# Two encoder layers on one core: gates through a logarithm, background steps at quarter tiles, an earlier operand split, and three narrow products for one projection

## The chip, the cores and the metric

The kernel runs on one core of a Trainium2 chip. The metric is the device time of one launch in microseconds (us). The kernel before takes 2427.96 us, the median of 3 runs (2427.77 to 2428.14).

## The reference, cut to what matters

Two layers of a bidirectional hybrid encoder work on 272 rows (16 meta rows and 256 tokens), model width 2048, in float32. Each layer is

```python
proj = h @ w_in          # gla q,k,v,r | low-rank decay | na q,k,v
o    = gated linear attention of q,k,v (4 heads, both directions)
o    = o * rsqrt(mean(o*o) + eps) * norm_w * silu(r)
y_na = neighbourhood attention (16 heads, softmax over a local window and the meta rows)
h    = LN(alpha*h + concat(o, y_na) @ w_out)
h    = LN(alpha*h + square(relu(h @ w_ff1)) @ w_ff2)
```

with `silu(r) = r / (1 + exp(-r))`. The meta rows are dropped at the end, so in layer two the columns that nothing else needs (gla q, r, na q and everything from the output projection on) are computed for 256 rows, not 272.

## The kernel before, in words

**Layout and products.** Activations lie with features on the 128 partitions and the 256 or 272 rows along the free axis. Each float32 matrix product is made of rounded parts: a weight chunk is split into a high part `wh` (a ScalarE cast, L147) and a low part `wl` (a VectorE subtraction, L148), an activation into `xh` and `xl`, and the sum is wh·xh + wh·xl + wl·xh. Weights stream from HBM in tiles of 128x1024, eight chunks each, issued by SyncE (L146) and always prepared two tiles ahead.

`by_m` (L190) makes one output tile of 128 features at a time: 16 chunks of 128 input features (32 in the second feed-forward product), each through `three` (L151). For 256 columns `three` issues two matmuls per chunk: wh against xh and xl side by side, 512 columns into a whole PSUM bank (L156), then wl against xh, 256 columns added to the right half (L157). The two halves of the bank must then be summed, in `whole` (L164): a ScalarE copy of the right half (L169), then a VectorE addition of the left half (L170), through the one buffer `jn`. For 272, 274 or 258 columns `three` issues three matmuls that add up in one region (L160 to L162), and nothing has to be summed.

**Two queues of side work.** While the big products run, generators are advanced by `pump` (L104): `fg` (foreground: silu of the gates, neighbourhood attention of a head pair, layer norm) and `bg` (background: gated linear attention). Each call adds credits and takes as many steps as whole credits are there. `by_m` calls it twice per tile, after chunk 8 and after the tile is taken out of PSUM; the rates of a call are `(1, GLA_R=1.3)` while the eight gate tiles `r` are made (L266) and `(1, GLA_NA=1.1)` during the 24 tiles of neighbourhood attention (L269). Before the last group of those, what is left of `bg` is run at once (L270). A planner (the tile framework's) lays the instructions of each engine in one order at build time; each engine runs its queue strictly in that order. Every side step's VectorE instructions are placed behind the newest `wl` (L98).

**Gated linear attention** (`gla`, L479) handles 4 heads, 10 levels each. One step of a level: TensorE multiplies the level's operands (L505, L498 and L500 for level 9) into a bank; the operands of the next level are made, an `Exp` on ScalarE (L471) and a multiplication on VectorE (L476, or L473 and L474); and GpSimd makes the differences for the level after that (`gaps`, four subtractions L460, or L447 to L450 for level 9). The buffers `lev` are three deep, so GpSimd may start a level's differences only when TensorE is through with the level three earlier. After the levels `gla_out` (L529) splits the 16 meta rows `Am` into the stack `am` (a memset L533 on GpSimd, two casts L214 on ScalarE, a subtraction L215 on VectorE) and, in its next steps, multiplies for each of two halves (L542 to L544, of which L544 reads `am`). Then come the mean of squares (L776), Newton's root and the output, which needs `gate`.

**Gates** (`ev_r`, L406, and `silu`, L417): ScalarE makes exp(-r) (L411), GpSimd adds 1 (L412), ScalarE copies r (L414); then three foreground steps: nothing, VectorE's reciprocal of each half (L421), and the product `gate` (L424). The buffers `rs` and `rv` are two deep.

Of the kernel before, what the change touches and what calls it, by code (L numbers as in the profile page):

```python
# [2 lines left out]

# [28 lines left out]
EPS = 1e-5  # L32
TAU = 16.0
NEG = -1e30
GLA_R, GLA_NA, NORMS = 1.3, 1.1, (1.0, 0.6)
LEAD = 4


# [9 lines left out]
class Trunk:  # L48
# [18 lines left out]
    def consts(self):  # L67
        nc, c = self.nc, self.cp
        t = lambda n, s, d=F32: c.tile(s, d, name=n, tag=n)
        self.vec = t("vec", [P, DEPTH, 66])  # L70
        nc.sync.dma_start(self.vec, self.i["vec"].rearrange("l p v -> p l v"))
        self.ident = t("ident", [P, P])
        nc.sync.dma_start(self.ident, self.i["ident"])
        self.sel = t("sel", [LRK, 2])
        nc.sync.dma_start(self.sel, self.i["sel"])
        self.qmask = t("qmask", [NM, NK2])
        nc.sync.dma_start(self.qmask, self.i["qmask"])
        self.mask = t("mask", [P, 7, P], U8)
# [12 lines left out]
        nc.gpsimd.memset(self.eps, EPS)  # L91
        self.one = t("one", [P, 1])
        nc.gpsimd.memset(self.one, 1.0)

# [53 lines left out]
            self.wl = nc.vector.tensor_tensor(wl[:, c], raw[:, c], wh[:, c].bitcast(F32), ALU.subtract).ins  # L148
        return wh, wl

    def three(self, ps, wh, wl, c, x, n, first, last):  # L151

        mm = self.nc.tensor.matmul
        xh, xl = x
        if n == T:
            mm(ps, lhsT=wh[:, c:c + P], rhs=x.both[:, :, :T], start=first, stop=False)  # L156
            mm(ps[:, T:], lhsT=wl[:, c:c + P], rhs=xh[:, :T], start=False, stop=last)  # L157
# [32 lines left out]
    def by_m(self, acts, ns, evict, pump=(0, 0), apart=False, renew=False):  # L190

        nk = len(acts)
        for m, n in enumerate(ns):
            ps = self.pm.tile([P, 512], F32, name="mm", tag="mm")
            for k in range(nk):
                if k % 8 == 0:
                    wh, wl = self.weights()
                self.three(ps, wh, wl, (k % 8) * P, acts[k], n, k == 0, k == nk - 1)
                if k % 8 == 7 and k < nk - 1:
                    self.pump(*pump)  # L200
                if renew and m == len(ns) - 1 and k == 8:
                    self.renew(2)
            parts = [ps[:, :T], ps[:, T:]] if n == T else [ps[:, :n]]
            evict(m, parts if apart else self.whole(parts))
            self.pump(*pump)

    def split(self, src, hi, lo):
        self.nc.scalar.copy(hi, src)
# [13 lines left out]
    def layer(self, l):  # L222
        nc, tc = self.nc, self.tc
        self.l = l
        self.full = l + 1 < DEPTH
        self.n = n = L if self.full else T
        with ExitStack() as actx:
            pool = lambda name, side, ctx=actx, bufs=1: ctx.enter_context(
                tc.tile_pool(name=name, bufs=bufs, side=side, reuse_waits="tile"))
            a = pool("att", "left")  # L230
            t = lambda nm, s: a.tile(s, F32, name=nm, tag=nm)
            self.qk = [t(f"qk{h}", [P, 2, L]) for h in range(GH)]
            self.be = [t(f"be{h}", [P, 2, L + 1]) for h in range(GH)]
            self.V = [t(f"V{i}", [P, GH * GDV]) for i in range(2)]
            self.VS = a.tile([80, GH * GDV], F32R, name="VS", tag="VS")
            nc.gpsimd.memset(self.VS.bitcast(F32), 0.0)
            self.y, self.gate, self.done = [None] * DC, {}, set()
            if l:
                self.by_m(self.x, [L + 2] * 4, lambda m, ps: self.fixed(self.ev_k, m, ps), pump=(1, NORMS[0]),
                          renew=True)  # L240
                first = self.by_k(self.x, L, self.normed)
                self.drain()
                self.lctx.close()
            else:
                with ExitStack() as ectx:
                    self.xr = pool("xr", "right", ectx)
                    for m, ps in enumerate(self.by_k(self.x, L, self.load_x, fine=True)):
                        self.ev_k(m, ps)
            with ExitStack() as ectx:
                self.ep = pool("early", "right", ectx)  # L250
                self.fcredit = 0
                self.fg.append(self.gates())
                if l == 0:
                    self.by_m(self.x, [L] * 4, self.ev_v, pump=(1, 0))
                else:
                    for m, ps in enumerate(first):
                        self.ev_v(m, ps)
                self.by_m(self.x, [n] * 4, self.ev_q, pump=(1, 0))
                self.by_m(self.x, [L] * 4, lambda m, ps: self.ev_v(4 + m, ps), pump=(1, 0))
                self.drain()  # L260
            self.a2 = pool("na", "left", bufs=2)
            with ExitStack() as gctx:
                self.credit = 0
                self.g2 = pool("gla", "right", gctx, 2)
                self.bg.append(self.gla())
                for g in range(2):  # L266
                    self.by_m(self.x, [n] * 4, lambda m, ps: self.ev_r(4 * g + m, ps), pump=(1, GLA_R))
                self.na_tiles()
                for g in range(6):  # L269
# [136 lines left out]
    def ev_r(self, c, ps):  # L406

        nc, n = self.nc, self.n
        self.y[c] = self.pair(self.yp, "y", c)
        s = self.g2.tile([P, L], F32, name="rs", tag="rs")[:, :n]  # L410
        nc.scalar.activation(s, ps, AF.Exp, scale=-1.0)  # L411
        nc.gpsimd.tensor_scalar(s, s, 1.0, 1.0, ALU.mult, ALU.add)  # L412
        r = self.g2.tile([P, L], F32, name="rv", tag="rv")[:, :n]
        nc.scalar.copy(r, ps)  # L414
        self.fg.append(self.silu(c, s, r))

    def silu(self, c, s, r):  # L417
        yield
        half = self.n // 2
        for p in (slice(0, half), slice(half, self.n)):  # L420
            self.nc.vector.reciprocal(s[:, p], s[:, p])  # L421
            yield
        gate = self.g2.tile([P, L], F32, name=f"gate{c}", tag=f"gate{c}", bufs=1)[:, :self.n]
        self.nc.vector.tensor_tensor(gate, r, s, ALU.mult)  # L424
        self.gate[c] = gate

    def newton(self, y, v, eps, t):
        nc = self.nc
# [50 lines left out]
    def gla(self):  # L479
# [11 lines left out]
        for h in range(GH):  # L491
            A = g2.tile([P, 6, P], F32, name="A", tag="A")
            Am = g2.tile([NM, L], F32, name="Am", tag="Am")
            for lv in levels:
# [19 lines left out]
                if lv == 9:  # L514
                    if full:
                        nc.vector.tensor_copy(A[:, 2:6:3, :NM], ps[:, T:T + 2 * NM].rearrange("p (s c) -> p s c", s=2))
                    nc.scalar.copy(Am[:, :T], ps[:NM, :T])
                elif lv >= 7:
                    nc.scalar.copy(A[:, 0:5:4, :] if lv == 7 else A[:, 1:4:2, :], p2)
                else:  # L520
# [6 lines left out]
            yield from self.gla_out(h, A, Am)  # L527

    def gla_out(self, h, A, Am):  # L529

        nc, n, g2 = self.nc, self.n, self.g2
        am = g2.tile([80, L], F32R, name="am", tag="am")[:, :n]
        nc.gpsimd.memset(am.bitcast(F32), 0.0)  # L533
        self.stack(Am[:, :n], am, NM, (0, 64), 32)
        yield
        af = A.rearrange("p s c -> p (s c)")
        os_ = []
# [485 lines left out]
```

## Time and profile before

| what | value |
|---|---|
| median of the runs | 2427.96 us |
| the profiled execution | 2427.82 us |
| its span, first to last instruction | 2425.8 us |
| mean granted TensorE clock | 0.997 |
| gate tiles, layer one / layer two, about | 113 to 171 us / 1345 to 1403 us |
| neighbourhood attention, layer one / layer two, about | 171 to 366 us / 1403 to 1591 us |
| `wl` subtractions L148, mean of 772 | 1226 ns |
| `wh` casts L147, mean of 772 | 1044 ns |

The profile has one page per execution and a trace that answers questions: a group of instructions by line, stretches of time with the busy time of each engine, and a timeline, whose rows are a start (us from the first instruction), a duration, an engine and line, the operation, and in brackets how long the engine had been idle and what ended that. Matmuls are pipelined, so their durations overlap: what a matmul costs is the distance from its start to the next one's start. All source lines named are those of the kernel before.

### The profile page before, as it was taken

What the parts mean: (1) busy time and instruction counts of PE and PEld (TensorE: products, weight loads), DVE (VectorE), ACT (ScalarE), POOL (GpSimd) and SP (SyncE); (2) the same over time, 40 slices, a digit from 0 to 9 for tenths busy, and PEclk for the clock granted to TensorE, in tenths of its full rate; (3) what the DMA queues carried; (4) which work ended last, traced back from release to release, by engine and by line L of the source; (5) the groups of instructions that cost most, each with busy time, mean ns of one, the idle gap of its engine ahead of it and who ended that gap; (6) DMA issues with size and microseconds to landing.
All of it is one profiled execution on the core that took longest, in us unless ns stands there. A gap on an engine that the chain in (4) does not pass through costs nothing.

```text
span 2425.8 us, 43082 instructions
## 1 busy us (share of the span) xinstructions
PE 2394.4 (99%) x17276; PEld 2270.6 (94%) x17276; DVE 1576.3 (65%) x2469; ACT 1189.2 (49%) x1962; POOL 285.7 (12%) x447
## 2 busy tenths in 40 slices
PE   9999999999999999999999999999999999999997
PEld 9999999999999999999999899999988888888886
DVE  6688777775544455546577787778866555666655
ACT  6555555564433344444456555555644333444443
POOL 1064420010000000000021444300200000000000
PEclk9999999999999999999999999999999999999998
DMA  7544444555555555555555444456566556556563
GB/s 243 165 133 155 145 133 158 172 179 175 174 175 174 175 177 174 177 175 173 176 168 186 144 156 150 136 156 191 184 190 184 190 189 187 189 185 189 186 189 129
DMA packets 118359, 417.46 MB, mean 172 GB/s; under 512 B 13388, under 2 KB 16332, under 8 KB 118160
## 3 DMA queue, kind: packets, MB, share of 16 engines
q1 hardware_dynamic: 118160, 414.72, 54.1%
q8 instruction: 135, 2.21, 0.4%
q14 instruction: 64, 0.52, 0.1%
HBM read 412.57 MB, written 2.10 MB: 171 GB/s over the span
## 4 chain that ended last, share of the span: by engine, by line
PE 94%; DVE 3%; issue 1%; ACT 1%; DMA 0%; POOL 0%; SPq 0%; ACTq 0%; DVEq 0%; POOLq 0%
PE mm L156 22%; PE mm L160 17%; PE mm L162 17%; PE mm L161 17%; PE mm L157 11%; PE mm L186 5%; PE bg L505 1%; DVE wl L148 1%; PE bg L652 1%; DVE acc L868 1%; PE bg L601 0%; POOL lev L460 0%; ACT wh L147 0%; PE bg L322 0%; PE bg L542 0%
## 5 line engine op out<-in xcount | busy, mean ns | idle before, releaser
L148 DVE TENSOR_TENSOR wl<-raw,wh 128x1024 fp32r<-128x1024 f32 (+1 forms) x772 | 946.0, 1226 | 654.6 <-ACT wh L147 646.2
L147 ACT CAST wh<-raw 128x1024 fp32r<-128x1024 f32 (+1 forms) x772 | 805.1, 1044 | 956.6 <-PE mm L161 405.6
L160 PE MATMUL mm<-x,wh 128*128 128x272 f32 (+2 forms) x2176 | 632.6, 291 | 0.0
L161 PE MATMUL mm<-x,wh 128*128 128x272 f32 (+2 forms) x2176 | 628.4, 289 | 0.0
L162 PE MATMUL mm<-x,wl 128*128 128x272 f32 (+2 forms) x2176 | 628.4, 289 | 0.0
L160 PEld LDWEIGHTS mm<-x,wh 128*128 128x128 f32 x2176 | 413.3, 190 | 1.4 <-issue 0.5
L162 PEld LDWEIGHTS mm<-x,wl 128*128 128x128 f32 x2176 | 410.6, 189 | 0.3
L161 PEld LDWEIGHTS mm<-x,wh 128*128 128x128 f32 x2176 | 410.0, 188 | 0.1
L156 PE MATMUL mm<-x,wh 128*128 128x512 f32 x1152 | 408.7, 397 | 0.0
L157 PE MATMUL mm<-x,wl 128*128 128x256 f32 x1152 | 324.5, 282 | 0.3 <-DVE wl L148 0.3
L156 PEld LDWEIGHTS mm<-x,wh 128*128 128x128 f32 x1152 | 217.7, 189 | 49.8 <-issue 0.6
L156 PE MATMUL mm<-y,wh 128*128 128x512 f32 x704 | 248.2, 393 | 0.1
L157 PEld LDWEIGHTS mm<-x,wl 128*128 128x128 f32 x1152 | 217.6, 189 | 0.8 <-DVE wl L148 0.8
L162 PE MATMUL mm<-y,wl 128*128 128x272 f32 x704 | 203.2, 289 | 0.0
L160 PE MATMUL mm<-y,wh 128*128 128x272 f32 x704 | 203.2, 289 | 0.0
L161 PE MATMUL mm<-y,wh 128*128 128x272 f32 x704 | 202.9, 288 | 0.0
L157 PE MATMUL mm<-y,wl 128*128 128x256 f32 x704 | 197.6, 281 | 0.5 <-DVE wl L148 0.5
L156 PE MATMUL mm<-u,wh 128*128 128x512 f32 x512 | 180.6, 393 | 0.0
L460 POOL TENSOR_TENSOR lev<-be 128x128 f32<-128x128 f32 (+1 forms) x256 | 151.9, 623 | 117.9 <-PE bg L505 49.8
L156 PEld LDWEIGHTS mm<-y,wh 128*128 128x128 f32 x704 | 131.8, 187 | 30.5 <-ACT wh L147 0.5
L162 PE MATMUL mm<-u,wl 128*128 128x272 f32 x512 | 147.8, 289 | 0.0
L160 PE MATMUL mm<-u,wh 128*128 128x272 f32 x512 | 147.8, 289 | 0.0
(234 smaller groups left out, 3327.9 us busy)
## 6 DMA issues: line engine op xcount, KB each, us to landing
raw<-in_wff SPq DMA_DIRECT2D x512, 512.0 KB, 3.6
raw<-in_win SPq DMA_DIRECT2D x190, 512.0 KB, 3.5
raw<-in_wout SPq DMA_DIRECT2D x64, 512.0 KB, 3.6
nb<-in_nab SPq DMA_DIRECT2D x16, 352.0 KB, 3.3
out<-acc SPq DMA_DIRECT2D x8, 256.0 KB, 2.2
xraw<-in_xT SPq DMA_DIRECT2D x7, 272.0 KB, 5.2
wraw<-in_wup SPq DMA_DIRECT2D x2, 392.0 KB
raw<-in_win SPq DMA_DIRECT2D x4, 128.0 KB, 2.8
```

The costliest lines, as they stand in the source:

```text
L147: nc.scalar.copy(wh[:, c], raw[:, c])
L148: self.wl = nc.vector.tensor_tensor(wl[:, c], raw[:, c], wh[:, c].bitcast(F32), ALU.subtract).ins
L156: mm(ps, lhsT=wh[:, c:c + P], rhs=x.both[:, :, :T], start=first, stop=False)
L157: mm(ps[:, T:], lhsT=wl[:, c:c + P], rhs=xh[:, :T], start=False, stop=last)
L160: mm(o, lhsT=wh[:, c:c + P], rhs=xh[:, :n], start=first, stop=False)
L161: mm(o, lhsT=wh[:, c:c + P], rhs=xl[:, :n], start=False, stop=False)
L162: mm(o, lhsT=wl[:, c:c + P], rhs=xh[:, :n], start=False, stop=last)
L186: self.nc.tensor.matmul(ps[m][:, :n], lhsT=parts[p][0][:, c:c + P], rhs=acts[j][parts[p][1]][:, :n], start=j + p == 0, stop=j == nk - 1 an ...
L460: tt = lambda o, x, y: nc.gpsimd.tensor_tensor(o, x, y, ALU.subtract)
L505: nc.tensor.matmul(ps[:, b], lhsT=k[:, b], rhs=q[:, r], start=True, stop=True)
L652: nc.tensor.matmul(r[hs], lhsT=(v2 if rest else v1)[:, t, hs], rhs=p2[:, t, :] if rest else p1[:, 2 * t + hh, :], start=rest, stop=not rest)
L868: return self.nc.vector.tensor_tensor(v, v, by[:, None, :].to_broadcast([P, m, n]), alu)
```

## The change

Five edits are made together. The gate takes another formula: with d = min(exp(-r), 1e38) + 1, a logarithm and an exponential on ScalarE give y, about 1/d, one Newton step on VectorE sharpens it, and r is copied with its sign turned so that the signs come out. `by_m` calls `pump` four times per tile: the background credit of a call is halved, the foreground keeps its two calls. `GLA_NA` goes from 1.1 to 1.25. The stack `am` is made in the step of level 9, one step earlier; the step it had stays as an empty one. And layer two's eight gate tiles take three products of 256 columns (`joint=False`) in place of 512 and 256, so that `whole` does nothing for them.

```diff
-GLA_R, GLA_NA, NORMS = 1.3, 1.1, (1.0, 0.6)
+GLA_R, GLA_NA, NORMS = 1.3, 1.25, (1.0, 0.6)
+BIG = 1e38
...
+        nc.gpsimd.memset(self.down, -64 * math.log(2))
...
     def three(...):
-        if n == T:
+        if once:
...
     def by_m(...):
+            once = joint and n == T
...
-                if k % 8 == 7 and k < nk - 1:
-                    self.pump(*pump)
+                if k % 8 == 3:
+                    self.pump(0, pump[1] / 2)
+                elif k % 8 == 7 and k < nk - 1:
+                    self.pump(pump[0], pump[1] / 2)
...
-            self.pump(*pump)
+            self.pump(pump[0], pump[1] / 2)
...
-                    self.by_m(self.x, [n] * 4, lambda m, ps: self.ev_r(4 * g + m, ps), pump=(1, GLA_R))
+                    self.by_m(self.x, [n] * 4, lambda m, ps: self.ev_r(4 * g + m, ps), pump=(1, GLA_R),
+                              joint=False)
...
     def ev_r(self, c, ps):
-        nc.scalar.activation(s, ps, AF.Exp, scale=-1.0)
-        nc.gpsimd.tensor_scalar(s, s, 1.0, 1.0, ALU.mult, ALU.add)
+        nc.scalar.activation(d, ps, AF.Exp, scale=-1.0)
+        nc.gpsimd.tensor_scalar(d, d, BIG, 1.0, ALU.min, ALU.add)
...
-        nc.scalar.copy(r, ps)
+        nc.scalar.activation(r, ps, AF.Copy, scale=-1.0)
...
     def silu(self, c, d, r):
         yield
-        for p in (slice(0, half), slice(half, self.n)):
-            self.nc.vector.reciprocal(s[:, p], s[:, p])
-            yield
-        self.nc.vector.tensor_tensor(gate, r, s, ALU.mult)
+        nc.scalar.activation(y, d, AF.Ln, scale=2.0 ** -64)
+        nc.scalar.activation(y, y, AF.Exp, scale=-1.0, bias=self.down)
+        yield
+        nc.vector.tensor_tensor(d, d, y, ALU.mult)
+        nc.vector.scalar_tensor_tensor(d, d, -2.0, y, ALU.add, ALU.mult)
+        nc.vector.tensor_tensor(y, d, r, ALU.mult)
...
     # in gla, the step of level 9; before: the first step of gla_out
                     nc.scalar.copy(Am[:, :T], ps[:NM, :T])
+                    am = g2.tile([80, L], F32R, name="am", tag="am")[:, :n]
+                    nc.gpsimd.memset(am.bitcast(F32), 0.0)
+                    self.stack(Am[:, :n], am, NM, (0, 64), 32)
```

In the built program this removes 32 reciprocals and 8 pairs of L169 and L170, adds 32 ScalarE activations and, net, 32 VectorE operations of two inputs, and adds 128 matmuls of 256 columns while 128 of 512 columns become 256 wide.

More of the change, by code (lines that the diff above doesn't have):

```diff
@@ L1 @@
+import math
 from collections import deque
@@ L91, in consts @@
         nc.gpsimd.memset(self.eps, EPS)
+        self.down = t("down", [P, 1])
+        nc.gpsimd.memset(self.down, -64 * math.log(2))
         self.one = t("one", [P, 1])
@@ L149, in made, with three @@
         return wh, wl
-    def three(self, ps, wh, wl, c, x, n, first, last):
+    def three(self, ps, wh, wl, c, x, n, first, last, once):
         mm = self.nc.tensor.matmul
         xh, xl = x
-        if n == T:
+        if once:
             mm(ps, lhsT=wh[:, c:c + P], rhs=x.both[:, :, :T], start=first, stop=False)
@@ L188, in by_k, with by_m @@
         return [p[:, :n] for p in ps]
-    def by_m(self, acts, ns, evict, pump=(0, 0), apart=False, renew=False):
+    def by_m(self, acts, ns, evict, pump=(0, 0), apart=False, renew=False, joint=True):
         nk = len(acts)
         for m, n in enumerate(ns):
+            once = joint and n == T
             ps = self.pm.tile([P, 512], F32, name="mm", tag="mm")
@@ L197, in by_m @@
                     wh, wl = self.weights()
-                self.three(ps, wh, wl, (k % 8) * P, acts[k], n, k == 0, k == nk - 1)
-                if k % 8 == 7 and k < nk - 1:
-                    self.pump(*pump)
+                self.three(ps, wh, wl, (k % 8) * P, acts[k], n, k == 0, k == nk - 1, once)
+                if k % 8 == 3:
+                    self.pump(0, pump[1] / 2)
+                elif k % 8 == 7 and k < nk - 1:
+                    self.pump(pump[0], pump[1] / 2)
                 if renew and m == len(ns) - 1 and k == 8:
                     self.renew(2)
-            parts = [ps[:, :T], ps[:, T:]] if n == T else [ps[:, :n]]
+            parts = [ps[:, :T], ps[:, T:]] if once else [ps[:, :n]]
             evict(m, parts if apart else self.whole(parts))
-            self.pump(*pump)
+            self.pump(pump[0], pump[1] / 2)
     def split(self, src, hi, lo):
@@ L409, in ev_r, with silu @@
         self.y[c] = self.pair(self.yp, "y", c)
-        s = self.g2.tile([P, L], F32, name="rs", tag="rs")[:, :n]
-        nc.scalar.activation(s, ps, AF.Exp, scale=-1.0)
-        nc.gpsimd.tensor_scalar(s, s, 1.0, 1.0, ALU.mult, ALU.add)
+        d = self.g2.tile([P, L], F32, name="rd", tag="rd")[:, :n]
+        nc.scalar.activation(d, ps, AF.Exp, scale=-1.0)
+        nc.gpsimd.tensor_scalar(d, d, BIG, 1.0, ALU.min, ALU.add)
         r = self.g2.tile([P, L], F32, name="rv", tag="rv")[:, :n]
-        nc.scalar.copy(r, ps)
-        self.fg.append(self.silu(c, s, r))
-    def silu(self, c, s, r):
+        nc.scalar.activation(r, ps, AF.Copy, scale=-1.0)
+        self.fg.append(self.silu(c, d, r))
+    def silu(self, c, d, r):
         yield
-        half = self.n // 2
-        for p in (slice(0, half), slice(half, self.n)):
-            self.nc.vector.reciprocal(s[:, p], s[:, p])
-            yield
-        gate = self.g2.tile([P, L], F32, name=f"gate{c}", tag=f"gate{c}", bufs=1)[:, :self.n]
-        self.nc.vector.tensor_tensor(gate, r, s, ALU.mult)
-        self.gate[c] = gate
+        nc = self.nc
+        y = self.g2.tile([P, L], F32, name=f"gate{c}", tag=f"gate{c}", bufs=1)[:, :self.n]
+        nc.scalar.activation(y, d, AF.Ln, scale=2.0 ** -64)
[4 more added lines that the diff above has]
+        nc.vector.tensor_tensor(y, d, r, ALU.mult)
+        self.gate[c] = y
     def newton(self, y, v, eps, t):
@@ L526, in gla, with gla_out @@
                 yield
-            yield from self.gla_out(h, A, Am)
-    def gla_out(self, h, A, Am):
+            yield from self.gla_out(h, A, am)
+    def gla_out(self, h, A, am):
         nc, n, g2 = self.nc, self.n, self.g2
-        am = g2.tile([80, L], F32R, name="am", tag="am")[:, :n]
-        nc.gpsimd.memset(am.bitcast(F32), 0.0)
-        self.stack(Am[:, :n], am, NM, (0, 64), 32)
         yield
```

## The prediction

> **What bounds the kernel now.** First the page's busy shares and its chain of waits:
>
> ```profile
> PE 2394.4 (99%) x17276; PEld 2270.6 (94%) x17276; DVE 1576.3 (65%) x2469; ACT 1189.2 (49%) x1962; POOL 285.7 (12%) x447
> ...
> PE 94%; DVE 3%; issue 1%; ACT 1%; DMA 0%; POOL 0%; SPq 0%; ACTq 0%; DVEq 0%; POOLq 0%
> ```
>
> TensorE (PE) sets the time; work taken off another engine pays only where PE waits. Second, the stretches in which the change acts (columns: length, then busy us of PE, PEld, DVE, ACT, POOL):
>
> ```profile
> 113.00:161.00 48.00, 46.94 (x370) 46.23 (x370) 37.90 (x55) 25.75 (x47) 30.17 (x44) 1.00 0.44 140
> ...
> 1353.00:1398.00 45.00, 41.33 (x244) 35.78 (x243) 36.54 (x53) 25.63 (x49) 25.34 (x44) 1.00 0.48 144
> ```
>
> PE is idle 1.1 us in layer one's gates and 3.7 us in layer two's. Third, the timeline at those holes. The largest:
>
> ```profile
> 1383.42 1.38 POOL L460 TENSOR_TENSOR lev<-be 128x128 f32<-128x128 f32 x1
> ...
> 1384.83 0.63 ACT L471 ACTIVATE lev<-lev 128x512 f32<-128x512 f32 x1 [1.75 <-POOL lev L460]
> 1384.83 0.59 PE L543 MATMUL bg<-A,V 128*128 128x256 f32 x2
> ...
> 1385.36 0.81 ACT L214 CAST am<-Am 16x256 fp32r<-16x256 f32 x2
> 1386.13 0.41 DVE L170 TENSOR_TENSOR jn<-jn,mm 128x256 f32<-128x256 f32 x1
> 1386.57 0.41 DVE L215 TENSOR_TENSOR am<-Am,am 16x256 fp32r<-16x256 f32 x1
> ...
> 1387.13 0.35 PE L544 MATMUL bg<-am,VS 80*128 80x256 f32 x1 [1.71 <-ACT rs L411]
> ```
>
> L544 waits for `am`, whose casts stand in ScalarE's queue behind an `Exp` of the next head, which waits for GpSimd; `jn` then stands in VectorE's queue ahead of the subtraction. (The profile names L411 as releaser; L215 ended last.) Other holes:
>
> ```profile
> 153.77 0.36 PE L544 MATMUL bg<-am,VS 80*128 80x272 f32 x1 [1.06 <-DVE am L215]
> ```
> ```profile
> 1369.89 0.68 PE L505 MATMUL bg<-lev 128*128 128x128 f32 x4 [1.02 <-DVE lev L476]
> ```
> ```profile
> 1380.48 0.67 PE L498 MATMUL bg<-lev 128*128 128x256 f32 x2 [0.60 <-ACT rv L414]
> ...
> 1381.72 0.39 PE L157 MATMUL mm<-x,wl 128*128 128x256 f32 x1 [0.34 <-DVE wl L148]
> ```
> ```profile
> 1447.16 0.84 PE L776 MATMUL bg<-sp,onesr 128*128 128x256 f32 x2 [0.77 <-ACT sp L208]
> ```
>
> The bracket understates a hole, since durations overlap. I price each by starts: first PE start after the side work minus last before it, less the same sequence where it is undisturbed. For L542 to L544 in layer two that is 3.05 against 1.11 us at 1390, so 1.94.
>
> **Sum of the holes**, in us: L544 at 152 1.30 and at 1385 1.94; the double step L505 at 1368 1.24; L498 at 1380 0.84, and the `wl` wait behind it 0.79; L505 at 1409 0.43; L776 at 1446 1.27, at 286 and 1513 together 0.66; L652 at 1535, where POOL is in the middle of 8.6 us of differences and `p` is late behind a `wl`, 0.88. Together 9.35 us: the ceiling of the gain. (I leave out holes at the starts of layers, under `w_out`, and a 0.24 us pause inside each L601 group: nothing here touches them.)
>
> **Part by part.**
>
> *Three narrow products.* Two starts per chunk become three. An L156/L157 chunk lasts 0.351 us (starts 1391.83, 1392.19, 1392.54). 256 columns in three products are not in the trace; the nearest rows are L186 with 256 columns, 0.118 a start, so 0.354 a chunk, and L160 to L162 with 258 columns, 0.3625. Over 128 chunks: +0.4 to +1.5 us on PE; I take +0.8, nearer to the row with the very width. What goes is 8 x (0.365 L169 + 0.414 L170), off PE's path, but `ev_r` starts about 1 to 1.5 us sooner after a tile (L169 at 1353.12, L170 only at 1354.39, L411 at 1354.8).
>
> *Logarithm.* Per tile VectorE loses two reciprocals (0.99 each at 136 columns, 0.94 at 128) and keeps a product (0.43); it gains a product (0.43) and a scalar-tensor-tensor (0.43, row L432): about -1.1 us, 16 times. ScalarE gains Ln and Exp, between 0.42 (L430) and 0.52 (L338) each: some +0.95 us, 16 times, less the eight L169. ScalarE is 54% to 57% busy in those stretches and ends near 70%, so PE sees neither as a sum. The new wait: Ln waits for POOL's addition (0.40 to 1.40, L412), and behind it in ScalarE's queue stand `wh` casts and level `Exp`s. In the built order each Ln comes behind an `Exp` whose POOL work precedes the addition, so that it waits for the addition alone; `wh` is prepared two tiles ahead. Cost 0; with that cover gone, up to 1.0 per tile. silu now needs two credits per tile where two arrive; before it needed three, and the backlog held `rs` back: evictions L411 ran to 1418.5, though the tiles end near 1403.
>
> *Quarter steps.* The same number of steps, rarely two together. A lone L505 step costs PE 0.36 plus 0.08 on the second product after it, two together 0.81 plus 0.08: the split itself is worth nothing. What it buys is distance: between level 9 and L542 stood 24 products of 0.125 in layer one (3.0 us) and 8 chunks in layer two (2.8 us); the built order now has 36 products (4.5 us; 4.25 in layer two). L776 likewise gets half as much again. The levels themselves keep their distances within a quarter tile, later rather than earlier.
>
> *Early stack.* In layer two the casts now stand ahead of the next head's `Exp`: the 1385 hole would need the stack to take over 4 us from `Am`, and its parts are 0.36 + 0.81 + 0.41. In layer one the built order still has the `Exp` first; the chain from level 9 to L544 took 5.0 us (148.8 to 153.8), and PE now arrives about 5.0 us after level 9: 0 to 0.3 left.
>
> *GLA_NA 1.25.* A tile of the attention stage lasts (1591-1403)/24 = 7.8 us; 2.5 steps per tile are one per 3.1 us, where 2.2 were one per 3.6. POOL's twelve differences at 1527.6 took 8.62 us, so 2.9 per level: it still fits, closely. New holes: 0 to 3; I take 0.8. The forced rest before the last group falls away; it shows no hole.
>
> *What goes.* L498's wait went through `jn`: the level's `Exp` ended at 1377.99, but VectorE did `jn` first (1379.22) and L473 after it. The double step at 1368 is now single, and POOL idled 1.06, 1.05 and 1.45 us there waiting for L411, which now comes sooner. I leave 0.3 at 152, 0.8 for 1368 to 1409, 0.1 at 1446, 0.5 at 1535, 0.3 for the two small ones: 2.0.
>
> Sum: -(9.35 - 2.0) + 0.8 + 0.8 = -5.75 on the profiled 2427.82, so **2422.1 us**; the median lies 0.14 higher. A difference of 0.2%, 4.9 us, is about what a measurement of this kernel can tell from no change.
>
> **The rivals.**
>
> *POOL is late anyway.* In the gate stage ten levels need 8 x 2.6 + 4.2 + 0.4 = 25.4 us of POOL (its rows from 1355 to 1382) and about 2.0 for four additions, against ten steps of 7.1/2.6, together 27.3 us of PE (a gate tile of layer two lasts (1402.5-1345.2)/8 = 7.1). For it: the holes at 1368 and 1380 begin with POOL. Against: two levels are prepared ahead. Half of the holes stay, 4.7, and 2 new: 2427.8 - 4.7 + 2.0 + 0.8 = 2425.9.
>
> *Slower, by the lock between VectorE and POOL.* A 128x128 difference takes 0.40 beside a reciprocal, but 1.38 beside a subtraction of two tensors that began first:
>
> ```profile
> 1381.59 0.94 DVE L421 RECIPROCAL rs<-rs 128x128 f32<-128x128 f32 x1
> ...
> 1381.90 0.40 POOL L460 TENSOR_TENSOR lev<-be 128x128 f32<-128x128 f32 x1
> ```
>
> The change trades reciprocals, beside which POOL runs on, for two two-tensor operations per tile, 0.86 us: 16 x 0.86 = 13.8 us of POOL. Its idle time among the levels of a head is 3.6 us (the gaps between 122 and 149); two such heads take 7.2. From there on it decides: 6.6 reaches PE, no hole goes, and 2427.8 + 6.6 + 0.8 = 2435.2. Against it: VectorE has as much less to do, so the operations can fall where POOL idles.
> [...]
>
> *The change doesn't act:* the planner undoes the new places. The built order shows the distances above; 2428.6 (only the +0.8) else.
>
> **Chances.** Forecast 0.60; late POOL 0.30; no effect 0.05; lock 0.05. The forecast runs from 2418.9 (all holes gone, +0.4) to 2423.1. Range 2418.9 to 2426.5, which leaves out the lock, no effect, and the tails. Faster by over 0.2% (under 2423.1) 0.60, within 0.2% 0.34, slower 0.06.
>
> **What would show it.** PE idle in layer two's gates under 1 us, no hole before the matmul that reads `am`; chunk starts 0.354 to 0.3625 apart; no reciprocal of 128 or 136 columns; VectorE's busy time there down by about 10 us. Wrong if POOL's differences grow past 2.9 us a level with PE waiting for them, or if `wh` casts start late behind Ln.

## The result and the profile after

The changed kernel takes **2452.45 us** (median of 4 runs, 2450.98 to 2454.62), the kernel before 2428.05 beside it: a ratio of 1.0101, with a 95% interval from 1.0084 to 1.0119. It is 24.4 us slower, where 5.7 us faster was forecast; the range ended at 2426.5. Two runs of the kernels further down stand far apart from the others of their kernel for a reason that no run here shows, 5172.70 us (undo_third_credit) and 2898.91 us (pace_log); the ratios leave them out.

From here on `after` is the changed kernel. Its lines have moved: `wh` is L151, `wl` L152, the three products L164 to L166, `jn` L173 and L174, the stack `am` L221 and L222, the gate's addition on GpSimd L420, Ln and Exp L430 and L431, differences L471 (level 9 L458 to L461), a level's Exp L482, its multiplication L487 (level 9 L484, L485), level matmuls L509 and L516, the copy of Am L528, `gla_out` L553 to L555, and in the attention pairs the softmax L593 to L599, the copies `v` and `nv` L637 and L640, `p` L652 and L653, its products L663. The page's busy shares and chain of waits:

```profile
PE 2403.1 (98%) x17404; PEld 2282.5 (93%) x17404; DVE 1562.5 (64%) x2461; ACT 1200.4 (49%) x1986; POOL 292.8 (12%) x448
...
PE 88%; issue 4%; DVE 3%; POOL 3%; ACT 1%; DMA 0%; SPq 0%; ACTq 0%; POOLq 0%; DVEq 0%
```

VectorE lost 13.8 us, ScalarE and GpSimd gained 11.2 and 7.1. But PE holds 88% of the chain where it held 94%: it waits longer, although no other engine has become the bound. The stage marks put all of the loss into gates and attention. In layer one they last from 113 to 379.83 us (before: to 366.98, so +12.85), in layer two the stretch from the low-rank product to the output projection grew from 290.85 to 304.07 (+13.22); the rest is equal within 1 us.

The gate stages (length, busy us of PE, PEld, DVE, ACT, POOL, granted clock, DMA share, GB/s); the second row is 11.6 us later than before's, as far as the stage has moved:

```profile
113.00:161.00 48.00, 44.90 (x350) 43.63 (x349) 33.00 (x55) 28.50 (x53) 31.39 (x43) 1.00 0.37 115
1364.60:1409.60 45.00, 41.89 (x341) 40.81 (x340) 34.77 (x51) 29.01 (x55) 31.57 (x44) 1.00 0.48 152
```

PE is idle 3.1 us in both rows (before: 1.1 and 3.7), although VectorE has 4.9 and 1.8 us less to do. What PE waits for over the whole span (total, times, longest):

```profile
PE bg L516 <- DVE nv L640: 5.6, 3, 3.3
...
PE bg L555 <- DVE am L222: 3.9, 2, 3.3
PE bg L663 <- DVE p L653: 3.9, 2, 2.7
PE bg L516 <- DVE lev L487: 2.8, 4, 1.0
```

Three of the four did not exist in this size: apart from one of 4.5 for a weight cast, no single wait of before is above 1.7 us. Priced as in the prediction, by starts less the undisturbed sequence, and now over all side work of the two stages, the holes sum to 2.96 + 6.70 in before and 14.74 + 17.73 in `after`. The largest of layer one, in the timeline:

```profile
205.13 0.88 DVE L593 TENSOR_REDUCE nst<-ns 128x4 f32<-128x704 f32 x1
...
206.04 0.44 ACT L595 ACTIVATE ns<-ns,nst 128x176 f32<-128x176 f32 x1 [2.83 <-DVE nst L593]
...
207.59 0.62 PE L554 MATMUL bg<-A,V 128*128 128x272 f32 x2
...
208.40 0.34 ACT L528 COPY Am<-bg 16x256 f32<-16x256 f32 x1
208.65 1.04 ACT L151 CAST wh<-raw 128x1024 fp32r<-128x1024 f32 x1
...
209.59 0.85 ACT L221 CAST am<-Am 16x272 fp32r<-16x272 f32 x2
209.72 1.23 DVE L152 TENSOR_TENSOR wl<-raw,wh 128x1024 fp32r<-128x1024 f32 x1 [0.32 <-ACT wh L151]
...
210.98 0.43 DVE L222 TENSOR_TENSOR am<-Am,am 16x272 fp32r<-16x272 f32 x1
...
211.55 0.56 PE L555 MATMUL bg<-am,VS 80*128 80x272 f32 x1 [3.35 <-DVE am L222]
```

Level 9 was multiplied at 201.3, but its `Am` is only copied at 208.40: in ScalarE's queue the six exponentials of an attention pair's softmax stand first, and they wait for that pair's maximum on VectorE. Then a weight cast, the stack, a `wl`, the last part of the stack. In before, that pair met the output step of the head and not its level 9, which stood at 199.66:

```profile
206.68 0.87 PE L601 MATMUL bg<-nk,nq 64*128 64x176 f32 x8
...
207.63 0.73 PE L542 MATMUL bg<-A,V 128*128 128x272 f32 x2
```

L601 makes a pair's scores; in `after` the same products start at 196.20, ahead of level 9. The second kind of hole:

```profile
1552.27 2.30 POOL L458 TENSOR_SCALAR lev<-be 128x256 f32<-128x256 f32 x1
...
1555.19 1.14 POOL L461 TENSOR_SCALAR lev<-be 128x256 f32<-128x256 f32 x1
...
1556.36 0.66 ACT L482 ACTIVATE lev<-lev 128x544 f32<-128x544 f32 x1 [3.42 <-POOL lev L461]
...
1556.92 1.03 ACT L151 CAST wh<-raw 128x1024 fp32r<-128x1024 f32 x1
...
1558.12 0.37 ACT L637 COPY v<-bg 128x256 f32<-128x256 f32 x1
1559.13 0.41 DVE L174 TENSOR_TENSOR jn<-jn,mm 128x256 f32<-128x256 f32 x1
1559.46 0.92 DVE L640 COPY nv<-bg 48x64 f32<-48x64 f32 x4
```

Level 9's Exp stands idle for 3.42 us at the head of ScalarE's queue; `v`, whose transposes ended at 1553.05, is copied at 1558.12, `nv` behind `wl` and `jn` at 1559.46, and PE's next level, which the profile lets wait for `nv`, at 1560.5. Third, the clock (same columns as above):

```profile
204.00:210.80 6.80, 4.21 (x31) 3.70 (x29) 4.78 (x15) 4.71 (x18) 2.12 (x7) 1.00 0.56 189
210.80:217.70 6.90, 6.15 (x25) 5.83 (x25) 4.57 (x12) 3.79 (x8) 0.00 (x0) 0.51 0.48 153
217.70:224.50 6.80, 6.80 (x65) 6.58 (x65) 2.72 (x6) 2.58 (x6) 1.47 (x3) 1.00 0.30 84
```

Behind the hole TensorE runs at half clock for 6.83 us. The clock's record has two more such stretches in these stages, 3.41 us each from 1453.3 and from 1511.3, and none in before. Together 13.65 us at half speed are up to 6.8 us lost.

### The profile page after: what moved, and what is told of

The parts are those of the page before. It is cut to its first block, busy times and chain, and to the rows that moved or that the text cites. A ratio compares the mean times of both kernels' runs of the same rounds, so it can differ in the third digit from the quotient of the medians.

```text
span 2451.6 us, 43341 instructions
## 1 busy us (share of the span) xinstructions
PE 2403.1 (98%) x17404; PEld 2282.5 (93%) x17404; DVE 1562.5 (64%) x2461; ACT 1200.4 (49%) x1986; POOL 292.8 (12%) x448
## 4 chain that ended last, share of the span: by engine, by line
PE 88%; issue 4%; DVE 3%; POOL 3%; ACT 1%; DMA 0%; SPq 0%; ACTq 0%; POOLq 0%; DVEq 0%
PE mm L160 20%; PE mm L164 16%; PE mm L166 16%; PE mm L165 16%; PE mm L161 11%; PE mm L190 5%; POOL lev L471 2%; DVE wl L152 1%; PE bg L516 1%; PE bg L663 1%; DVE acc L879 1%; ACT wh L151 1%; PE bg L612 0%; PE bg L330 0%; PE bg L553 0%
## 5 line engine op out<-in xcount | busy, mean ns | idle before, releaser
L152 DVE TENSOR_TENSOR wl<-raw,wh 128x1024 fp32r<-128x1024 f32 (+1 forms) x772 | 945.5, 1225 | 681.3 <-ACT wh L151 662.6
L151 ACT CAST wh<-raw 128x1024 fp32r<-128x1024 f32 (+1 forms) x772 | 805.5, 1043 | 956.1 <-PE mm L165 408.8
L164 PE MATMUL mm<-x,wh 128*128 128x272 f32 (+3 forms) x2304 | 671.6, 291 | 0.0
L166 PE MATMUL mm<-x,wl 128*128 128x272 f32 (+3 forms) x2304 | 665.1, 289 | 0.6 <-DVE wl L152 0.6
L165 PE MATMUL mm<-x,wh 128*128 128x272 f32 (+3 forms) x2304 | 665.0, 289 | 0.0
L164 PEld LDWEIGHTS mm<-x,wh 128*128 128x128 f32 x2304 | 438.1, 190 | 2.0 <-issue 0.9
L166 PEld LDWEIGHTS mm<-x,wl 128*128 128x128 f32 x2304 | 435.4, 189 | 1.1 <-DVE wl L152 0.8
L165 PEld LDWEIGHTS mm<-x,wh 128*128 128x128 f32 x2304 | 434.9, 189 | 0.1
L160 PE MATMUL mm<-x,wh 128*128 128x512 f32 x1024 | 362.7, 396 | 0.0
L161 PE MATMUL mm<-x,wl 128*128 128x256 f32 x1024 | 288.3, 282 | 0.1
L160 PEld LDWEIGHTS mm<-x,wh 128*128 128x128 f32 x1024 | 193.3, 189 | 44.9 <-issue 0.8
L166 PE MATMUL mm<-y,wl 128*128 128x272 f32 x704 | 203.1, 288 | 0.0
L164 PE MATMUL mm<-y,wh 128*128 128x272 f32 x704 | 203.1, 288 | 0.0
L161 PE MATMUL mm<-y,wl 128*128 128x256 f32 x704 | 197.5, 281 | 0.5 <-DVE wl L152 0.5
L471 POOL TENSOR_TENSOR lev<-be 128x128 f32<-128x128 f32 (+1 forms) x256 | 151.1, 622 | 93.5 <-DVE be L355 47.3
L166 PE MATMUL mm<-u,wl 128*128 128x272 f32 x512 | 147.7, 289 | 0.0
L164 PE MATMUL mm<-u,wh 128*128 128x272 f32 x512 | 147.7, 288 | 0.0
```

What stands on the lines that cost most here:

```text
L151: nc.scalar.copy(wh[:, c], raw[:, c])
L471: tt = lambda o, x, y: nc.gpsimd.tensor_tensor(o, x, y, ALU.subtract)
```

## The experiments

Every kernel was timed in three rounds beside the kernel before. "Holes" is the sum over both stages as above (before: 9.7, `after`: 32.5).

### Four theories, one part undone at a time

**A**: the gate now takes two foreground credits, not three; the backlog goes, the attention pairs start earlier and meet other levels. **B**: GpSimd's addition in its new form (minimum, add) is slow (in `after` 1.56 us at the mean of 256 columns, in before 0.49), and Ln waits for it. **C**: 2.5 level steps per attention tile are too many as a rate. **D**: the lock of the prediction, GpSimd held up beside VectorE's operations on two tensors (a difference of 128x128 in before took 1.38 us at the median when it began under a `wl`, 0.40 under a reciprocal).

The third credit:

```diff
     def silu(self, c, d, r):
         yield
+        yield
```


> The changed kernel with an empty foreground step put back into silu, so that a gate again takes three credits where two arrive. Theory A (the vanished backlog lets the neighbourhood-attention pairs start earlier, and their softmax meets level 9 and the stack): the waits before the matmul that reads am at 207 and 1449 go, with the half clock behind them, and most of the loss with them: 2430 to 2436. Theory B (the addition in the form min, add is slow on GpSimd, and Ln waits for it): about 2446 to 2452. Theory C (2.5 level steps per attention tile are too many): no change, 2450.

Measured: 2445.93, ratio to before 1.0073 [1.0056, 1.0090], holes 24.5. The holes before `am` at 207 and 1449 fell from 3.75 to 0.63 and from 2.96 to nothing, as A has it, but others opened: a pair's products and a level at 250, 3.06, with half a clock behind. A is a part, 6.5 us. That the credit decides when the pairs start can be read from all twenty profiles: the first pair's scores start between 194.1 and 197.5 in the ten kernels whose gate takes two credits, and between 206.4 and 213.0 in the ten where it takes three.

The form of the addition:

```diff
-nc.gpsimd.tensor_scalar(d, d, BIG, 1.0, ALU.min, ALU.add)
+nc.gpsimd.tensor_scalar(d, d, 1.0, 1.0, ALU.mult, ALU.add)
```


> The changed kernel with the gate's addition in the form of before, multiply by 1 and add 1, in place of minimum with 1e38 and add 1; it leaves out the clamp, which no input here reaches. Theory B: the addition falls from 1.1 to 1.9 us to about 0.4, the holes at 142 to 153 and 1382 to 1393 (some 8 us together) go, Ln no longer holds up the stack: 2436 to 2444. Theory A: the collisions at 207 and 1449 stay, 2446 to 2452. Theory C: 2450.

Measured: 2449.78, 1.0091 [1.0076, 1.0106], holes 29.4. The first hole, at 142, is gone (0.91), its two successors shrink by 0.4 to 0.5 each. B is worth 2.7 us here, less than the 3.6 us between the fastest and the slowest run of `after`.

The pace:

```diff
-GLA_R, GLA_NA, NORMS = 1.3, 1.25, (1.0, 0.6)
+GLA_R, GLA_NA, NORMS = 1.3, 1.1, (1.0, 0.6)
```


> The changed kernel with 1.1 in place of 1.25 background steps per half tile in the attention stage. Theory C: the holes from 270 to 330 and from 1479 to 1584 go, about 12 us with the half clock at 1511: 2438 to 2442. Theory A: the levels move against the pairs, so that single holes move, but the sum stays within 6 us: 2446 to 2456. Theory B: 2450.

Measured: 2433.90, 1.0025 [1.0016, 1.0035], holes 15.5. More than C had asked for: 18.6 of the 24.4 us, and the holes at 207 and 1449 go as well.

The gate of before put back in `ev_r` and `silu` (reciprocals, three credits, multiply and add on GpSimd), everything else as in `after`:

```diff
-        nc.scalar.activation(y, d, AF.Ln, scale=2.0 ** -64)
-        nc.scalar.activation(y, y, AF.Exp, scale=-1.0, bias=self.down)
...
+            self.nc.vector.reciprocal(s[:, p], s[:, p])
```


> The changed kernel with the gate's reciprocals of before, in two halves and with three credits; quarter steps, early stack, 1.25 and the narrow products stay. Theories A and B: 2426 to 2434. Theory C, or quarter steps that do harm: 2440 or above. Theory D (the lock between a VectorE operation on two SBUF tensors and GpSimd): 2430, but then undo_third_credit and undo_min each change less than 4 us.

Measured: 2442.94, 1.0062 [1.0047, 1.0077], holes 20.1. Less than A, B and D said (15 us stay), and about the sum of the two single edits, 6.5 + 2.7 = 9.2 against 9.5. C had the right side.

### Is it GpSimd's lead, the quarters, or the rate?

**E**, new: a level's Exp is issued one step behind its differences; at quarters two steps can be 1.95 us apart, often less than GpSimd needs for a level (in `after` 1.47 to 4.81 from the first to the end of the fourth subtraction, for level 9 2.91 to 4.36). Three levels ahead instead of two:

```diff
-        t = self.g2.tile([P, 2, L], F32, name="lev", tag="lev", bufs=3)
+        t = self.g2.tile([P, 2, L], F32, name="lev", tag="lev", bufs=4)
...
-        begun = [self.gaps(*next(todo)) for _ in range(2)]
+        begun = [self.gaps(*next(todo)) for _ in range(3)]
```


> The changed kernel with GpSimd's differences begun three levels ahead instead of two (four lev buffers; am and Am get one buffer each to make room). Theory E, formed on the first four runs (2.5 steps per tile at quarters often come one quarter, 1.95 us, apart, which is less than the 2.6 to 5.2 us that GpSimd takes for a level; the level's Exp then waits at the head of ScalarE's queue, and weight casts and attention copies behind it): the holes at levels and at the attention's copies go, 2424 to 2436. Theory C (2.5 steps per tile are too many for GpSimd and VectorE as a rate): the wait only comes later, 2444 or above. Theory A (early pairs): 2442 to 2450.

To make room, `am` and `Am` have one buffer each in this kernel instead of two; what that costs was not measured apart.

Measured: 2453.24, 1.0105 [1.0090, 1.0120]: no gain. E falls as the cause of the whole, though the single buffers may hide a part of a gain. Of the gate stages' holes at levels, those at 142, 1388 and 1393 did go (holes 26.3). But the attention's stayed or grew (5.63 at 1505), a pair's scores now wait for copies behind GpSimd's longer queue (1.26 at 195, 2.07 at 1435), and the half clock came five times, 20.5 us in all.

Steps at halves again:

```diff
-                if k % 8 == 3:
-                    self.pump(0, pump[1] / 2)
-                elif k % 8 == 7 and k < nk - 1:
-                    self.pump(pump[0], pump[1] / 2)
+                if k % 8 == 7 and k < nk - 1:
+                    self.pump(*pump)
```


> The changed kernel with background steps at halves of a tile, as before; 1.25, logarithm, early stack and narrow products stay. Theory E: most steps are a half tile apart again, 2430 to 2440. Theory C, the rate: no better, 2446 or above. Theory A: 2444 to 2450.

Measured: 2444.67, 1.0072 [1.0055, 1.0088], holes 24.4, without any half clock. Between E and C, so neither.

The pace alone, on the kernel before (1.25 for 1.1, as in the diff above, the other way round):

> The kernel before with 1.25 in place of 1.1 and nothing else. Theory E: 2426 to 2434, since steps stay at halves. Theory C, the rate: 2438 or above.

Measured: 2432.69, 1.0020 [1.0011, 1.0029], holes 15.1. Alone 1.25 costs 4.9, in `after` 18.6: not a price of its own.

The changed kernel with 1.1 and reciprocals (the diffs of undo_pace and undo_log together):

> The changed kernel with 1.1 and with the gate's reciprocals of before: quarter steps, early stack and narrow products alone. Theory E: few steps are one quarter apart at 1.1, 2423 to 2430. If the logarithm and the minimum are the rest of undo_pace's 6 us (theory B), the holes at 142 to 153 shrink to about 1.5 us: 2428 or below. If quarter steps as such do harm: 2432 or above.

Measured: 2429.89, 1.0009 [0.9999, 1.0018], holes 11.6. Quarters, early stack and narrow products gain nothing together.

### Rate or meeting

**F**, formed on these: what counts is which step of an attention pair falls beside which level, since their copies and exponentials stand in one ScalarE and one VectorE queue, in the order issued. Every edit that shifts the steps against each other moves all meetings. Then the time is no line in the pace.

```diff
-GLA_R, GLA_NA, NORMS = 1.3, 1.25, (1.0, 0.6)
+GLA_R, GLA_NA, NORMS = 1.3, 1.2, (1.0, 0.6)
```


> The changed kernel with 1.2 in place of 1.25. Theory C, the rate: on the line through 1.1 (2433.9) and 1.25 (2452.5), 12.4 us per 0.1, so 2446. Theory F, formed on the runs so far (what counts is which level falls together with which step of an attention pair, since their copies and exponentials stand in one ScalarE and one VectorE queue): 1.2 moves every meeting, so the time leaves the line by over 6 us here or at 1.3.

Measured: 2444.83, 1.0066 [1.0050, 1.0083], on C's line (2446).

The same with 1.3 in place of 1.2:

> The changed kernel with 1.3 in place of 1.25. Theory C, the rate: 2458 on the line through 1.1 and 1.25. Theory F: no line; 2436 to 2450, with other holes than at 1.25, unless 1.2 has left it already.

Measured: 2440.03, 1.0052 [1.0037, 1.0067]: more steps per tile, yet 12 us faster than `after` and 18 below the line. C falls. At 1.3 the hole at 1556 is absent and the one at 207 is 1.57; instead 3.47 opens at 316 and 2.49 at 1548, where the pair's products meet the output step.

The level before the pair where both fall on one place:

```diff
     def pump(self, fg, bg):
-        self.fcredit += fg
-        while self.fcredit >= 1:
-            self.step(self.fg, 1)
-            self.fcredit -= 1
         self.credit += bg
...
+        self.fcredit += fg
+        while self.fcredit >= 1:
+            self.step(self.fg, 1)
+            self.fcredit -= 1
```


> The changed kernel with the two halves of pump exchanged: where a level and a step of an attention pair fall on one place, the level is issued first. Theory F: the softmax exponentials no longer stand ahead of the copy of Am, the holes before the matmul that reads am at 207 and 1449 (3.75 and 2.96, with the half clock behind them) go, 2436 to 2446. Theory C, the rate: 2449 or above.

Measured: 2442.28, 1.0060 [1.0045, 1.0075], holes 19.0, no half clock. The time is in F's range, the mechanism only half: the weight cast no longer stands between the copy of Am and the stack, and the idle time before `am` at 207 falls from 3.35 to 1.53. But the planner still placed the four long exponentials ahead of the copy of Am, and at 1443 the hole stayed (3.09).

### Each part alone, on the kernel before

The early stack:

```diff
                     nc.scalar.copy(Am[:, :T], ps[:NM, :T])
+                    am = g2.tile([80, L], F32R, name="am", tag="am")[:, :n]
+                    nc.gpsimd.memset(am.bitcast(F32), 0.0)
+                    self.stack(Am[:, :n], am, NM, (0, 64), 32)
```


> The kernel before with the early stack and nothing else. As predicted for that part: the hole of 1.94 at 1385 goes, the one of 1.30 at 152 keeps at least half: 2425 to 2427. If the stack in the level's step harms what stands behind it on ScalarE (a weight cast, the next Exp): 2429 or above.

Measured: 2427.48, 1.0000 [0.9991, 1.0009], holes 9.7. The hole at 1384 is unchanged, 1.90: the part does nothing. In the source the `Exp` of the next head is issued in the same step, ahead of the stack, and ScalarE's queue still has it there: `Am` is copied at 1382.52, the Exp begins at 1384.63 after 1.75 us of waiting for GpSimd, and the casts follow at 1385.17.

The narrow products (`once` and `joint=False` as in the change):

```diff
-        if n == T:
+        if once:
...
-lambda m, ps: self.ev_r(4 * g + m, ps), pump=(1, GLA_R))
+lambda m, ps: self.ev_r(4 * g + m, ps), pump=(1, GLA_R), joint=False)
```


> The kernel before with three products of 256 columns in layer two's gates and nothing else. The prediction's term: +0.4 to +1.5, so 2428.0 to 2429.2, no new hole. Theory F: the evictions come some 1 us sooner and can move a meeting by as much either way, 2427 to 2430.

Measured: 2427.02, 0.9994 [0.9984, 1.0003], holes 7.3. The holes at 1368 and 1446 shrink from 1.34 to about 0.46 each, the one at 1380 goes, the one before `am` grows from 1.89 to 2.42 and brings 3.41 us of half clock.

The logarithm (`ev_r` and `silu` of the change):

```diff
+        nc.gpsimd.tensor_scalar(d, d, BIG, 1.0, ALU.min, ALU.add)
...
+        nc.scalar.activation(y, d, AF.Ln, scale=2.0 ** -64)
```


> The kernel before with the gate from a logarithm and nothing else: halves, 1.1, late stack. The prediction's term (cost 0, the cover holds): 2426 to 2428. Theories B and F (the addition with a minimum takes 1.1 us or more of GpSimd's queue, and the pairs start earlier): holes at levels and before am in the gate stages, 2430 to 2436.

Measured: 2439.53, 1.0047 [1.0032, 1.0062], holes 18.4, 10.2 us of half clock: the dearest part alone, 11.6 us. The hole before `am` at 152 is 2.87 instead of 1.30. Its timeline (L416 is the addition, L426 Ln, L218 and L219 the stack, L549 to L551 the output):

```profile
152.49 1.33 DVE L152 TENSOR_TENSOR wl<-raw,wh 128x1024 fp32r<-128x1024 f32 x1
...
152.60 0.36 ACT L524 COPY Am<-bg 16x256 f32<-16x256 f32 x1 [0.43 <-DVE A L523]
...
152.83 1.97 POOL L416 TENSOR_SCALAR rd<-rd 128x272 f32<-128x272 f32 x1
...
154.83 0.43 ACT L426 ACTIVATE gate<-rd 128x272 f32<-128x272 f32 x1 [1.87 <-POOL rd L416]
155.17 0.84 ACT L218 CAST am<-Am 16x272 fp32r<-16x272 f32 x2
...
156.18 0.57 PE L551 MATMUL bg<-am,VS 80*128 80x272 f32 x1 [2.31 <-DVE am L219]
```

`Am` is ready at 152.96, but Ln stands ahead of the casts and waits 1.87 us for the addition.

The quarters (the diff of undo_quarters, the other way round):

> The kernel before with background steps at quarters and nothing else. The prediction's term (a greater distance from level 9 to am): 2424 to 2426. Theory F: the holes only move, 2427 to 2431; from pace_log less the narrow products: 2429.2.

Measured: 2429.98, 1.0008 [0.9999, 1.0018], holes 11.1. The holes at 1368 and 1409 go, the one before `am` in layer two falls from 1.89 to 0.39, as predicted. But in layer one, which had few, level 9 gets 0.57 at 145, its output keeps 1.18, and a pair's transposes meet level 9 at 262 (1.21). In layer two PE idles longer ahead of level 9, 1.14 us at 1382 where before had 0.60 at 1380.

Three levels ahead, on the kernel before (the diff of lead3):

> The kernel before with GpSimd's differences begun three levels ahead (four lev buffers, one am and one Am). In lead3 the holes at levels of the gate stages went and those at the attention's copies stayed. Here the holes of 1368, 1380, 1384 and 1409 (4.6 us) shrink: 2423 to 2426. If only the meetings count: 2427 to 2430.

Measured: 2432.63, 1.0020 [1.0011, 1.0030], holes 12.3: slower, with 3.50 before `am` and 6.83 us of half clock behind it. Here too `am` and `Am` have one buffer each, and this was not tried apart.

### What the logarithm pays for

log_only with the addition as multiply and add (the diff of undo_min):

> log_only with the addition as multiply by 1 and add 1, without the clamp at 1e38. Theory B: the addition takes 0.4 in place of 1.07 to 1.97, Ln follows at once, and the holes of log_only before am at 152 and 1394 (2.87, 3.31) and at the double levels (1.45, 3.35) fall back to those of before: 2428 to 2432. If the logarithm's other parts (two more ScalarE activations per tile, fewer credits) carry the loss: 2435 to 2440.

Measured: 2435.82, 1.0034 [1.0022, 1.0046], holes 16.6, no half clock. 3.7 of the 11.6 us go. The same place as above:

```profile
151.51 0.77 POOL L416 TENSOR_SCALAR rd<-rd 128x272 f32<-128x272 f32 x1 [0.58 <-ACT rd L415]
...
152.25 0.70 PE L549 MATMUL bg<-A,V 128*128 128x272 f32 x2 [0.96 <-DVE A L523]
...
152.41 0.43 ACT L426 ACTIVATE gate<-rd 128x272 f32<-128x272 f32 x1
...
153.96 0.36 PE L551 MATMUL bg<-am,VS 80*128 80x272 f32 x1 [0.55 <-DVE am L219]
```

The addition takes 0.77 and is done before `Am`. Ln waits for nothing, and PE's idle time before the matmul that reads `am` falls from 2.31 to 0.55. Not all of that is won: PE now idles 0.96 us before L549, for `A`, so both waits together are 1.51.

And with the third credit (the diff of undo_third_credit):

> log_mult with an empty foreground step in front, so that a gate takes three credits as with reciprocals. If the earlier foreground steps carry what log_mult leaves: 2427 to 2429, and below log_mult by 2 or more. If not: as log_mult, within 1.5.

Measured: 2431.76, 1.0017 [1.0008, 1.0027], holes 11.8. Another 4.1 us. What remains, 4.2, lies in the main at two output steps (151: 2.00, 1386: 3.61, then 6.83 us of half clock). At 151 PE waits 0.97 us for `A` before it waits 0.55 for `am`; at 1386 Ln, the gate's Exp and its three products stand in the two queues ahead of the stack. That these are the reason was read from the order, not tried.

## Why the prediction was wrong, point by point

| part | forecast | alone | undone in `after` |
|---|---|---|---|
| narrow products | +0.8, and -1.2 with the `jn` wait | -0.9 | |
| early stack | most of 1.94 | -0.2 | |
| quarters | distance, most of 1.30 and 1.24 | +2.1 | -7.8 |
| 1.25 | +0.8 | +4.9 | -18.6 |
| logarithm | 0 | +11.6 | -9.5 |
| all | -5.7 | sum +17.5 | `after` +24.4 |

Each difference is against the median measured beside it, those in the last column against `after`. The first three parts alone can't be told from no change: their intervals hold 1. The sum of the parts leaves 7 us, which is about what the intervals of the six differences leave open together. That the parts act on one another is clearer from single ones: 1.25 costs 4.9 alone and 18.6 in `after`.

**The step that failed first: the logarithm at cost 0.** It rested on a cover, "it waits for the addition alone", and took that addition at L412's 0.40 to 1.40, the row of another pair of operations. The new form takes (256 columns, alone) 1.07 where L412 took 0.40, and its 16 executions took 25.5 us in `after` where L412's took 11.8. Ln waited for it 14 times, 18.8 us in all; in the timeline of log_only above the stack stands behind Ln. The text named a price for the case without cover, up to 1.0 per tile, and the part alone cost 11.6 / 16 = 0.73; but that this fits is in part luck, since 4.1 of the 11.6 came with the third credit, and up to 5.1 are half clock, neither of which was in that price. It should have stood in the range.

**The second: the claim that a gate needs two credits where two arrive.** The claim is true, and was written down as a relief. What it leaves out is who comes next in that queue: the attention pairs, which then start some 10 us earlier. Giving the third credit back is worth 6.5 us in `after`, 4.1 in log_mult.

**The third: GLA_NA 1.25 at 0.8.** It compared averages, 2.9 us of GpSimd per level against one step per 3.1. GpSimd did not become late: ScalarE waited 65.4 + 29.2 us for differences in `after`, 78.5 + 28.8 in before. What changed, in the two timelines of `after` above, is what stood behind those waits. So the rival of the late GpSimd is not what happened either, and neither is a rate: 1.2, 1.25 and 1.3 give 2444.8, 2452.5 and 2440.0.

**The fourth: that holes only go.** The sum took each hole of before as something to remove and gave new ones 0.8. Holes are where two steps happen to meet, and before had few. Of its 9.35, the quarters and the narrow products, each alone, did shrink those of 1368 and 1446; but the edits opened others elsewhere. What should have been priced is that any two steps can meet, and that such a meeting cost 1 to 4 us in most of these kernels, 5.6 at the most (lead3 at 1505).

**The half clock** was in no term: before's record shows full clock from 8.86 to 2411.84 us. It is up to 6.8 of the 24.4 us.

**The lock** of the prediction, by which the new VectorE operations would add 13.8 us to GpSimd's work, did not show there: GpSimd's differences took 191.9 us in before and 189.4 in `after`, summed over all levels. Single differences are held up beside VectorE: in before, of those of 128x128, the 28 that began under a `wl` took 1.38 us at the median and ended 0.25 to 0.32 after it, the 21 that began under a reciprocal took 0.40 at the median. The addition is lengthened in the same way. In `after`, 11 of its 16 executions began under a `wl`; they ended 0.92 to 0.99 us after that and took up to 2.11, the other five 1.07 to 1.20. In the timeline of log_only above the addition begins at 152.83 under a `wl` that ends at 153.82 and finishes 0.98 later, near the 1.12 that it takes for 272 columns with VectorE idle (`after` at 156.44). Why GpSimd is held up was not shown. What is left of log_only without minimum and with three credits, 4.2 us, is what the added activations, products and this lock cost together, if the parts add up.

**Right**: the third product (starts 0.118 apart in a chunk, 0.356 between chunks at the median, in the range 0.354 to 0.3625), the end of the wait through `jn`, the distance from quarters at L544 in layer two (1.94 to 0.31 in `after`), no reciprocals left. Of the signs named for being right, two did not come: PE was idle 3.1 us in layer two's gate window (under 1 forecast), and VectorE's busy time there fell by 1.8 us (about 10). Of the signs named for being wrong, Ln holding up the queue came true, though it was the stack more than the weight casts that stood behind it.

What stays open: which of the meetings at 1.25 belong to the pace and which to the shifted pairs, since undoing either moves both; and whether another order of issue could hold the gains of quarters and narrow products without the new holes. No kernel tried is faster than before by more than the measurement tells; the nearest is narrow_only, 0.9994 [0.9984, 1.0003].

## What to carry to other kernels

Where generators share in-order queues, price a change of pace or of credits by who will stand behind whom at the longest waits, not by the average load of an engine: a bound, here of 1 to 4 us per meeting, on either side belongs in the range. An edit that takes away one queue's backlog starts the next work in it earlier; follow that work as if it were part of the change. And price an added instruction by its own operations, since the same tile with another pair of them took 1.07 instead of 0.40.

## What the runs showed of the hardware

GpSimd's time for the same tile changed with the pair of operations. Here is the gate's addition on 128 partitions by 256 columns, first in before (multiply, add), then in log_only (minimum, add); behind the bar stand its busy time in us and the mean of one in ns:

```profile
L412 POOL TENSOR_SCALAR rs<-rs 128x256 f32<-128x256 f32 x8 | 3.9, 488 | 44.3 <-ACT rs L411 44.3
```
```profile
L416 POOL TENSOR_SCALAR rd<-rd 128x256 f32<-128x256 f32 x8 | 10.0, 1256 | 53.5 <-ACT rd L415 53.4
```

These means include the executions that a VectorE operation held up; the shortest took 0.40 us in before, and with the minimum 1.07 in `after`.

In the gate and attention stages TensorE's half clock came in stretches of 3.41 or 6.83 us only, and within a profile they begin on one grid of 3.413 us (in `after` at 210.80, 1453.25 and 1511.28, which are 364 and 17 such steps apart). Worked out from the records of the twelve profiles that have such stretches: in the 28 windows of that grid that end where a stretch begins, PE's matmuls filled 0.15 to 1.88 us, and of the windows not followed by half clock only four are as empty, the emptiest with 1.53 and 1.64. So no single long wait was needed: in the fullest of the 28 (lead3 before 146.9) PE was idle for 1.53 us, in two waits of 0.77. Nor did half clock follow every such window, as the four show: the emptiest of them holds a part of a wait of 3.34 that lies across two windows (`after` at 1557, 1.53 and 1.95 us filled). What else decides it was not shown.
